# A channel shuffle on one core: tiles of 32 KB a partition, permuted in place through PSUM, from one pool of six buffers

## The chip, the cores and the metric

One core of a Trainium2 chip. The metric is device time in microseconds (us) of one execution. Each kernel was run several times; medians are quoted. All profiled runs are with granted clock 1.00. The kernel's tiles lie in two on-chip memories, SBUF and PSUM, over 128 partitions. "Row" below means one pixel of 256 channels, 1 KB in float32. A tile of q rows a partition holds 128 x q rows, so a tile of 24 rows is 3 MB and one of 8 rows is 1 MB.

## The reference

```python
batch, h, w, c = 16, 64, 64, 256
groups = 8
x = x.reshape(batch, h, w, groups, c // groups)
x = x.transpose(0, 1, 2, 4, 3)          # (group, channel) -> (channel, group)
return x.reshape(batch, h, w, c).astype(np.float32)
```

Inside every row of 256 values, an 8 x 32 matrix is transposed. 67.1 MB are read and 67.1 MB written. Rows are independent, so a kernel may place them on partitions as it likes.

## The kernel before

SyncE issues the loads. VectorE permutes the first half of the rows of a tile, and ScalarE the second half, from an input tile to an output tile in SBUF. ScalarE's queue issues the stores. There are four input and four output buffers of 24 KB a partition.

```python
_SIZES = [24] * 21 + [8]
_IN_BUFS = 4
_OUT_BUFS = 4
_SHARES = (("vector", 1), ("scalar", 1))
# ... cut: set-up, rows(), permute() ...
    for q in _SIZES:
        in_tile = in_pool.tile([P, biggest * c], F32, name="in_tile")
        nc.sync.dma_start(out=in_tile[:, : q * c], in_=rows(x_flat, first, q))
        out_tile = out_pool.tile([P, biggest * c], F32, name="out_tile")
        # ... cut: VectorE permutes the first half, ScalarE the second ...
        nc.scalar.dma_start(out=rows(out_flat, first, q), in_=out_tile[:, : q * c])
        first += P * q
```

`rows()` gives each partition q consecutive rows. So for each partition a DMA moves one contiguous run of q KB, and the trace records each run as one packet: in each of the two queues 2,688 packets of 24,576 B and 128 of 8,192 B, for 21 tiles of 24 rows and one of 8. The counts of the queues further below also hold 352 records of 4 B, of 9 ns each.

## Time and profile before

| | before |
|---|---|
| time, median of 3 | 317.53 us |
| span of the profiled run | 316.0 us |
| packets of loads and stores, share of 16 engines' time | 49.8% + 49.3% |
| VectorE, ScalarE busy | 65.3, 118.9 us |
| last load landed, last store issued | 302.4, 304.3 us |

From the page: busy time of the engines; the DMA row, which has the busy tenths of the DMA engines in 40 slices of the span (9 is 90% or more); and the queues (packets, MB, share). Queue q1 carries the loads and q10 the stores.

```profile
DVE 65.3 (21%) x22; ACT 118.9 (38%) x23; POOL 0.2 (0%) x4
...
DMA  8999999999999999999999999999999999999996
...
q1 hardware_dynamic: 3168, 67.11, 49.8%
q10 hardware_dynamic: 3168, 67.11, 49.3%
```

DMA is full from the second slice to the last but one. No compute engine is near that. From the view of waits (us in total, times, longest):

```profile
DVE out_tile L51 <- DMA in_tile<-in_x_dram: 238.3, 22, 11.6
ACT out_tile L49 <- DMA in_tile<-in_x_dram: 184.6, 22, 9.2
```

Both compute engines wait for loads only. From the groups by shape (count, then busy us, mean ns of one; then idle us before them and its releaser):

```profile
L49 ACT COPY out_tile<-in_tile 128x3072 f32<-128x3072 f32 x21 | 115.7, 5510 | 180.3 <-DMA in_tile<-in_x_dram 180.3
L51 DVE COPY out_tile<-in_tile 128x3072 f32<-128x3072 f32 x21 | 64.2, 3058 | 231.6 <-DMA in_tile<-in_x_dram 231.6
L49 ACT COPY out_tile<-in_tile 128x1024 f32<-128x1024 f32 x1 | 1.9, 1937 | 4.3 <-DMA in_tile<-in_x_dram 4.3
...
L51 DVE COPY out_tile<-in_tile 128x1024 f32<-128x1024 f32 x1 | 1.1, 1095 | 6.7 <-DMA in_tile<-in_x_dram 6.7
```

From the difference of the two shapes, a strided copy costs VectorE (3,058 - 1,095) / 2,048 = 0.96 ns an element and ScalarE (5,510 - 1,937) / 2,048 = 1.74 ns. By windows (start:end and length in us, busy us of each engine and instructions in brackets, clock, DMA share, GB/s):

```profile
core 0: us, DVE busy (x) ACT busy (x) POOL busy (x), PEclk, DMA share, GB/s
60.00:280.00 220.00, 47.01 (x16) 83.46 (x16) 0.00 (x0) 1.00 1.00 432
...
302.00:308.00 6.00, 1.09 (x1) 1.94 (x1) 0.00 (x0) 1.00 1.04 446
308.00:310.00 2.00, 0.00 (x0) 0.00 (x0) 0.00 (x0) 1.00 0.97 418
310.00:312.00 2.00, 0.00 (x0) 0.00 (x0) 0.00 (x0) 1.00 0.85 360
312.00:314.00 2.00, 0.00 (x0) 0.00 (x0) 0.00 (x0) 1.00 0.87 369
314.00:316.00 2.00, 0.00 (x0) 0.00 (x0) 0.00 (x0) 1.00 0.01 4
```

The middle moves 432 GB/s with DMA at 1.00.

### The profile page before, as it was taken

How to read it: one execution, taken by the hardware profiler on the slowest of the kernel's cores; microseconds unless marked ns; L12 is line 12 of the kernel's file. 1: busy time of each engine (PE TensorE's matmuls, PEld its weight loads, DVE VectorE, ACT ScalarE, POOL GpSimd, SP SyncE). 2: the span in 40 equal slices, each digit the busy share in tenths (PEclk: the TensorE clock that was granted, in tenths of full speed). 3: DMA queues.
4: the chain of work that ended last, by engine and by line, in shares of the span. 5: the costliest groups of instructions: out<-in, count | busy, mean ns of one | idle time of the engine just before them, and what ended most of it. 6: DMA issues, size and time to landing. Idle time of an engine off the chain costs nothing.

```text
span 316.0 us, 236 instructions
## 1 busy us (share of the span) xinstructions
DVE 65.3 (21%) x22; ACT 118.9 (38%) x23; POOL 0.2 (0%) x4
## 2 busy tenths in 40 slices
DVE  0440321303030303113030303031220303030310
ACT  1681624425160606243351606061533426060620
POOL 0000000000000000000000000000000000000000
DMA  8999999999999999999999999999999999999996
GB/s 302 439 395 426 426 445 432 420 442 439 417 439 445 417 436 442 426 426 445 426 423 445 439 414 442 442 417 439 442 421 432 442 420 432 442 429 429 421 446 291
DMA packets 6337, 134.23 MB, mean 425 GB/s; under 512 B 704, under 2 KB 704, under 8 KB 704
## 3 DMA queue, kind: packets, MB, share of 16 engines
q1 hardware_dynamic: 3168, 67.11, 49.8%
q10 hardware_dynamic: 3168, 67.11, 49.3%
q14 instruction: 1, 0.01, 0.0%
HBM read 67.11 MB, written 67.11 MB: 425 GB/s over the span
## 4 chain that ended last, share of the span: by engine, by line
another core or an unknown queue 43%; DMA 32%; ACT 20%; ACTq 1%; issue 0%
DMA in_tile<-in_x_dram 32%; ACT out_tile L49 20%; ACTq L66 1%; ACTq L49 0%
## 5 line engine op out<-in xcount | busy, mean ns | idle before, releaser
L49 ACT COPY out_tile<-in_tile 128x3072 f32<-128x3072 f32 (+1 forms) x22 | 117.7, 5348 | 184.6 <-DMA in_tile<-in_x_dram 184.6
L51 DVE COPY out_tile<-in_tile 128x3072 f32<-128x3072 f32 (+1 forms) x22 | 65.3, 2968 | 238.3 <-DMA in_tile<-in_x_dram 238.3
L49 ACT ACT_TABLE_LOAD x1 | 1.3, 1283 | 0.7 <-PEq L84 0.7
L84 POOL MEMSET const-bfloat16-1.0<- 128x1 bf16 x1 | 0.1, 102 | 0.0
L84 POOL MEMSET const-uint8-127<- 128x1 uint8 x1 | 0.1, 102 | 0.0
L84 POOL MEMSET const-float32-1.0<- 128x1 f32 x1 | 0.1, 99 | 0.0
L84 POOL MEMSET const-float32-0.0<- 128x1 f32 x1 | 0.1, 98 | 0.2 <-issue 0.2
## 6 DMA issues: line engine op xcount, KB each, us to landing
in_tile<-in_x_dram SPq DMA_DIRECT2D x21, 3072.0 KB, 52.6
out_dram<-out_tile ACTq DMA_DIRECT2D x21, 3072.0 KB, 20.2
in_tile<-in_x_dram SPq DMA_DIRECT2D x1, 1024.0 KB, 47.9
out_dram<-out_tile ACTq DMA_DIRECT2D x1, 1024.0 KB, 10.4
```

Of the source, the lines that this page charges most:

```text
L49: nc.scalar.copy(out=dst, in_=src)
L51: getattr(nc, engine).tensor_copy(out=dst, in_=src)
L66: nc.scalar.dma_start(out=rows(out_flat, first, q), in_=out_tile[:, : q * c])
L84: nc = _bacc.Bacc("TRN2", target_bir_lowering=False, num_devices=1)
```

## The change

The intent: larger tiles, hence fewer and larger DMAs, in the same 192 KB of SBUF a partition (8 x 24 and 6 x 32). For that each tile is permuted in place: VectorE permutes eight rows at a time into PSUM, and ScalarE copies them back over the input. An 8-row tile at the start and small ones at the end are to shorten head and tail.

```diff
-_SIZES = [24] * 21 + [8]
-_IN_BUFS = 4
-_OUT_BUFS = 4
+_SIZES = [8] + [32] * 14 + [24, 8, 8, 8, 8]
+_BUFS = 6
-_SHARES = (("vector", 1), ("scalar", 1))
+_PIECE = 8
 # ... cut: pools; permute() removed; the order of instructions is now that of the program ...
     for q in _SIZES:
-        in_tile = in_pool.tile([P, biggest * c], F32, name="in_tile")
-        nc.sync.dma_start(out=in_tile[:, : q * c], in_=rows(x_flat, first, q))
-        out_tile = out_pool.tile([P, biggest * c], F32, name="out_tile")
-        # ... cut ...
-        nc.scalar.dma_start(out=rows(out_flat, first, q), in_=out_tile[:, : q * c])
+        buf = pool.tile([P, biggest * c], F32, name="buf")
+        nc.sync.dma_start(out=buf[:, : q * c], in_=rows(x_flat, first, q))
+        for k in range(0, q, _PIECE):
+            piece = buf[:, k * c : (k + _PIECE) * c]
+            bounce = psum.tile([P, _PIECE * c], F32, name="bounce")
+            nc.vector.tensor_copy(
+                out=bounce.rearrange("p (i j g) -> p i j g", j=CPG, g=G),
+                in_=piece.rearrange("p (i g j) -> p i j g", g=G, j=CPG),
+            )
+            nc.scalar.copy(out=piece, in_=bounce)
+        nc.scalar.dma_start(out=rows(out_flat, first, q), in_=buf[:, : q * c])
```

Tiles are numbered from 0: tile 0 has 8 rows, tiles 1 to 14 have 32, tile 15 has 24, and tiles 16 to 19 have 8.

More of the change, by code (lines that the diff above doesn't have):

```diff
@@ L36 @@
     out_flat = out.rearrange("b h w c -> (b h w c)")
-    in_pool = ctx.enter_context(tc.tile_pool(name="in_pool", bufs=_IN_BUFS))
-    out_pool = ctx.enter_context(tc.tile_pool(name="out_pool", bufs=_OUT_BUFS))
+    pool = ctx.enter_context(tc.tile_pool(name="pool", bufs=_BUFS))
+    psum = ctx.enter_context(
+        tc.tile_pool(name="psum", bufs=2, space=bass.MemoryType.PSUM)
+    )
     def rows(flat, first, q):
         return flat[first * c : (first + P * q) * c].rearrange("(p f) -> p f", p=P)
-    def permute(engine, dst, src):
-        src = src.rearrange("p (i g j) -> p i j g", g=G, j=CPG)
-        dst = dst.rearrange("p (i j g) -> p i j g", j=CPG, g=G)
-        if engine == "scalar":
-            nc.scalar.copy(out=dst, in_=src)
-        else:
-            getattr(nc, engine).tensor_copy(out=dst, in_=src)
+    ctx.enter_context(tc.manual_schedule(engines=None))
     first = 0
     for q in _SIZES:
-        in_tile = in_pool.tile([P, biggest * c], F32, name="in_tile")
-        nc.sync.dma_start(out=in_tile[:, : q * c], in_=rows(x_flat, first, q))
-        out_tile = out_pool.tile([P, biggest * c], F32, name="out_tile")
-        at, total = 0, sum(n for _, n in _SHARES)
-        for k, (engine, n) in enumerate(_SHARES):
-            last = k == len(_SHARES) - 1
-            upto = q if last else min(q, at + -(-q * n // total))
-            if upto > at:
-                cols = slice(at * c, upto * c)
-                permute(engine, out_tile[:, cols], in_tile[:, cols])
-            at = upto
-        nc.scalar.dma_start(out=rows(out_flat, first, q), in_=out_tile[:, : q * c])
+        buf = pool.tile([P, biggest * c], F32, name="buf")
[6 more added lines that the diff above has]
+                in_=piece.rearrange("p (i g j) -> p i j g", g=G, j=CPG),
+            )
+            nc.scalar.copy(out=piece, in_=bounce)
+        nc.scalar.dma_start(out=rows(out_flat, first, q), in_=buf[:, : q * c])
         first += P * q
```

## The prediction

> **What bounds the kernel now.** The 16 DMA engines do, from end to end. The page's DMA row reads 9 in all slices but the first and last; the two queues' packets fill 49.8% + 49.3% = 99.1% of the 316.0 us span (queue table). By windows, 60 to 280 us moves 432 GB/s at DMA share 1.00, while VectorE is busy 47 and ScalarE 83 of those 220 us. Both idle only for loads (238 and 185 us, view of waits). [...]
>
> The packet records show the rest: a 24,576 B packet takes 912 ns, an 8,192 B one 309 ns. Hence 36.8 ns per KB (435 GB/s over 16 engines) plus about 7.5 ns a packet. The traffic, 67.1 MB in and 67.1 MB out, needs 308.7 us at that slope. Per engine: 352 packets x 7.5 ns = 2.6 us and 44 completion packets x 9 ns = 0.4 us. About 1.7 us is lost in slow packets at the start and where the first stores join. [...]
>
> **What the change does.** The bytes stay.
> - DMA: 20 loads and 20 stores instead of 22 and 22; 320 packets an engine instead of 352. Saves 32 x 7.5 + 4 x 9 = about 0.3 us, all on the path.
> - VectorE permutes everything: 64 pieces of 2,048 elements. Today (groups by form) 3,072 take 3,058 ns and 1,024 take 1,095: 0.96 ns an element. [...] I expect up to twice today's slope: 2.2 to 4.1 us a piece, best guess 4.0, in all about 255 us. Off the path: a 32-row tile costs DMA 2 x 8 x 1.21 = 19.4 us, VectorE 16 us.
> - ScalarE: strided copy (1.75 ns an element) becomes a contiguous one from PSUM, about 1.9 us a piece, 120 us in all; today 119. Off the path.
> - The latency from landing to store rises from 5.5 to about 18 us a full tile. It holds one of six buffers; the other five keep a load or a store queued, so DMA should not starve.
> - Head: the 8-row first tile lets stores begin near 10 us instead of 17, but loads already fill DMA then.
> - Tail: 24, 8, 8, 8, 8 keeps the last permutations (about 4 + 2 us each) under stores still queued; worth a few tenths at most.
>
> **Sum.** 317.5 - 0.3 (packets) - 0.1 (tail) = **317.1 us**, range 315.7 to 319.3. Chances: faster by over 2% 0.01, within 2% 0.95, slower 0.04.
>
> **What would show each step.** DMA share 1.00 and 432 to 434 GB/s in the middle; 32 KB packets near 1,214 ns; VectorE busy 140 to 260 us; ScalarE 115 to 130 us; the DMA row 9 throughout.
>
> **What would make it wrong.** A VectorE piece above about 4.8 us: VectorE would then need over 308 us and bound the kernel. Load and store queues both empty at times (DMA digit under 9 mid-run), because six shared buffers and the long landing-to-store latency starve them: slower. Faster would need a packet cost or a start loss that I have misread.

The range for a piece on VectorE (one to two times today's 0.96 ns an element, best guess 4.0 us), and with it 140 to 260 us, was the author's guess, and so was the 1.9 us of ScalarE: no run had shown a copy into or out of PSUM yet. The loss in slow packets comes to 1.6 us an engine by the packet records (their time beyond 912 and 309 ns each).

## More of the kernel before

The end is the part to remember: DMA stays near full until about 314 us. The timeline shows why (start, length, engine and line, operation; in brackets the idle time before it and its releaser; ACTq is ScalarE's queue issuing a DMA):

```profile
302.35 1.94 ACT L49 COPY out_tile<-in_tile 128x1024 f32<-128x1024 f32 x1 [4.29 <-DMA in_tile<-in_x_dram]
302.41 2.25 ACTq L66 DMA_DIRECT2D out_dram<-out_tile  x2
302.52 1.09 DVE L51 COPY out_tile<-in_tile 128x1024 f32<-128x1024 f32 x1 [6.70 <-DMA in_tile<-in_x_dram]
```

The last load lands at 302.35 us. After 1.94 us of ScalarE its store can be issued (the two issues in the line of 302.41 are those of the last two tiles, the later one at 304.3 us). By the packet records some 5 MB of stores are still to be moved when the load lands and some 4 MB when that store is issued, so the wait for the last tile's permutation is hidden.

## The result, and the profile after

| | before | after |
|---|---|---|
| time, median of 6 | 317.56 us | 319.85 us (319.63 to 320.71) |
| ratio of fast runs, 95% interval | | 1.0074 (1.0061 to 1.0087) |
| span of the profiled run | 316.0 us | 317.8 us |
| packets' share | 49.8% + 49.3% | 49.4% + 49.0% |
| VectorE, ScalarE busy | 65.3, 118.9 us | 228.2, 120.7 us |
| last load landed, last store issued | 302.4, 304.3 us | 307.6, 313.2 us |

A ratio here is the mean time of one kernel's fast runs over that of the other's in the same rounds, so it is not quite the ratio of the medians.

The change is 0.7% slower: inside "the same within 2%", but above the top of the predicted range, 319.3 us. The same lines of the page:

```profile
DVE 228.2 (72%) x64; ACT 120.7 (38%) x65; POOL 0.2 (0%) x4
...
DMA  8999999999999999999999999999999999999995
...
q1 hardware_dynamic: 2880, 67.11, 49.4%
q10 hardware_dynamic: 2880, 67.11, 49.0%
```

The packets took less time than before: 98.4% of 317.8 is 312.7 us an engine, against 99.1% of 316.0, or 313.2 us. So DMA did its work about 0.5 us faster (0.3 us was forecast), and the span is still 1.8 us longer. DMA stood still for about 2.3 us more than before. The groups and the waits:

```profile
L54 DVE COPY bounce<-buf 128x2048 f32<-128x2048 f32 x64 | 228.2, 3633 | 83.0 <-DMA buf<-in_x_dram 83.0
L58 ACT COPY buf<-bounce 128x2048 f32<-128x2048 f32 x64 | 119.4, 1865 | 186.9 <-DVE bounce L54 186.9
```

```profile
ACT buf L58 <- DVE bounce L54: 186.9, 64, 9.7
DVE bounce L54 <- DMA buf<-in_x_dram: 83.0, 18, 7.9
```

A piece takes VectorE 3,633 ns and ScalarE 1,865 ns. VectorE still waits for loads for 83 us in all, so it does not bound the kernel. The windows show where DMA stood still:

```profile
60.00:280.00 220.00, 166.27 (x47) 86.55 (x47) 0.00 (x0) 1.00 1.00 434
...
302.00:308.00 6.00, 3.96 (x2) 1.62 (x1) 0.00 (x0) 1.00 1.00 423
308.00:310.00 2.00, 2.00 (x1) 0.24 (x1) 0.00 (x0) 1.00 0.75 315
310.00:312.00 2.00, 1.26 (x1) 0.71 (x1) 0.00 (x0) 1.00 0.80 328
312.00:314.00 2.00, 0.00 (x0) 1.16 (x1) 0.00 (x0) 1.00 0.00 0
314.00:316.00 2.00, 0.00 (x0) 0.00 (x0) 0.00 (x0) 1.00 1.05 434
316.00:318.00 2.00, 0.00 (x0) 0.00 (x0) 0.00 (x0) 1.00 0.22 90
```

In the middle DMA moves 434 GB/s, a little more than before. From 308 us on its share is 0.75, 0.80 and then 0.00: from 312 to 314 us nothing is moved at all. Adding 1 - share times the length over all windows from 290 us to the end gives 4.6 us of standing still, against 2.5 us before (the last window counted to the end of the span; the window from 290 to 302 us, with shares 0.96 and 0.99, is counted in this and not shown). The timeline of the end:

```profile
294.22 3.60 DVE L54 COPY bounce<-buf 128x2048 f32<-128x2048 f32 x1 [7.92 <-DMA buf<-in_x_dram]
...
302.75 3.60 DVE L54 COPY bounce<-buf 128x2048 f32<-128x2048 f32 x1 [4.93 <-DMA buf<-in_x_dram]
...
307.64 3.62 DVE L54 COPY bounce<-buf 128x2048 f32<-128x2048 f32 x1 [1.29 <-DMA buf<-in_x_dram]
308.27 0.34 ACTq L59 DMA_DIRECT2D out_dram<-buf  x1
311.29 1.86 ACT L58 COPY buf<-bounce 128x2048 f32<-128x2048 f32 x1 [3.05 <-DVE bounce L54]
313.19 0.34 ACTq L59 DMA_DIRECT2D out_dram<-buf  x1
```

The last load lands at 307.6 us, 5.3 us later than before. Then come VectorE (3.62 us), ScalarE (1.86 us) and the store's issue at 313.19 us. The store of the tile before was issued at 308.27 us and has only 1 MB, so the stores run dry while the last tile is permuted.

Why does the last load land so late? The packet records of the trace are of each packet its start, length, queue and size. Packets of 8, 24 and 32 KB take 309, 912 and 1,213 ns (medians) in both directions. From first packet to last, the loads of tiles 16 to 19 (1 MB each) take 11.6, 11.3, 8.9 and 5.2 us, one right behind the other. Estimated from these times, a 1 MB load of 8 packets an engine would need 8 x 0.309 = 2.5 us with the engines to itself, and 4.9 us with half of their time. (The last 1 MB store, with no other transfer beside it, took 2.7 us.) Between 270 and 290 us after the first load packet, loads started 224 packets and stores 208, but these were 1.8 MB of loads and 6.7 MB of stores: in this stretch the two queues got nearly equal numbers of packets, not equal bytes. One 8 KB packet for each 32 KB packet would give 8 x (0.309 + 1.213) = 12.2 us for a 1 MB load, again an estimate from the packet times. That is near the 11.6 us seen.

### The profile page after: what moved, and what is told of

Its sections match the earlier page's. It is cut to its first block, busy times and chain, and to the rows that moved or that the text cites. A ratio compares the mean times of both kernels' runs of the same rounds, so it can differ in the third digit from the quotient of the medians.

```text
span 317.8 us, 277 instructions
## 1 busy us (share of the span) xinstructions
DVE 228.2 (72%) x64; ACT 120.7 (38%) x65; POOL 0.2 (0%) x4
## 3 DMA queue, kind: packets, MB, share of 16 engines
q1 hardware_dynamic: 2880, 67.11, 49.4%
q10 hardware_dynamic: 2880, 67.11, 49.0%
## 4 chain that ended last, share of the span: by engine, by line
DVE 59%; DMA 23%; another core or an unknown queue 15%; issue 1%; ACT 1%; SPq 0%; DVEq 0%
DVE bounce L54 59%; DMA buf<-in_x_dram 13%; DMA out_dram<-buf 9%; ACT buf L58 1%; SPq L50 0%; DVEq L54 0%
## 5 line engine op out<-in xcount | busy, mean ns | idle before, releaser
L54 DVE COPY bounce<-buf 128x2048 f32<-128x2048 f32 x64 | 228.2, 3633 | 83.0 <-DMA buf<-in_x_dram 83.0
L58 ACT COPY buf<-bounce 128x2048 f32<-128x2048 f32 x64 | 119.4, 1865 | 186.9 <-DVE bounce L54 186.9
```

Of the source, the lines that this page charges most:

```text
L54: nc.vector.tensor_copy(out=bounce.rearrange("p (i j g) -> p i j g", j=CPG, g=G), in_=piece.rearrange("p (i g j) -> p i j g", g=G, j=CPG),)
L58: nc.scalar.copy(out=piece, in_=bounce)
```

## The experiments

Three theories were set against each other.

- Theory A: loads and stores take turns packet by packet. The small tiles at the end are loaded in 8 KB packets against 32 KB store packets, so they come in slowly while the stores are used up quickly. The last load lands late, the stores run dry, and the permutation of the last tile (3.6 + 1.9 us) stands bare.
- Theory B: the long way from landing to store (about 16 us for a full tile), with six shared buffers, starves DMA in the middle, or the longer serial permutation alone is the cause.
- Theory C: the last load is late because its buffer comes free late. Its load is issued only at 280.2 us, when the store of tile 13 has landed.

Each kernel is the changed one with the edit shown, unless said otherwise. Times are medians, and the ratio in brackets is to the kernel before in the same rounds.

### Stores of tiles 13 to 15 cut into DMAs of 8 rows

```diff
-        nc.scalar.dma_start(out=rows(out_flat, first, q), in_=buf[:, : q * c])
+        dst = rows(out_flat, first, q)
+        step = _PIECE if t >= 13 else q
+        for k in range(0, q, step):
+            cut = slice(k * c, (k + step) * c)
+            nc.scalar.dma_start(out=dst[:, cut], in_=buf[:, cut])
```

> The change as it is, but the stores of tiles 13, 14 and 15 are issued as DMAs of 8 rows, so their packets are 8 KB like those of the last four loads. Theory A (packet-fair sharing delays the last small loads behind 32 KB store packets, so the last load lands at 307.6 us, the stores run dry and DMA idles about 2.2 us before the last store): loads of tiles 16 to 19 take about 5 us of traffic each instead of 9 to 11.5, the last load lands before 297 us, no DMA gap near 312 us, time 319.85 - 2.7 + 0.6 (64 more packets an engine at 7.5 ns, and more completions) = about 317.8. Theory B (only the length of the serial permutation at the end, or starvation in the middle by the long landing-to-store latency): the gap stays, time 320 to 320.5.

Measured 317.93 us (1.0012). By the packet records the last four loads took 4.7, 5.1, 5.8 and 5.3 us instead of 11.6 to 5.2, and DMA has share 1.02 from 312 to 314 us where the changed kernel has 0.00. The loss is gone, as theory A has it. One thing had not been foreseen: ScalarE was held up once for 24.5 us. The view of waits puts this to the landing of a load; the reading is that a store had to wait until a load on the same completion counter had landed (see the run with a buffer of its own for the last tile). So the experiment was repeated in a cleaner form at the end of this section.

### The last tile permuted by one VectorE copy in SBUF

```diff
+        if t == len(_SIZES) - 1:
+            last = last_pool.tile([P, q * c], F32, name="last")
+            nc.vector.tensor_copy(out=<last, permuted>, in_=<buf, strided>)
+            nc.scalar.dma_start(out=rows(out_flat, first, q), in_=last)
+            break
```

> The change as it is, but the last 8-row tile is permuted by one VectorE copy into an 8 KB SBUF buffer of its own and stored from there. Chain from the last landing to the store shortens from 5.5 us (3.63 + 1.86) to about 2.1 us. Theory A and the serial-chain rival alike: the 2.2 us DMA gap before the last store closes, time about 317.6; the last load still lands near 307.5. If the loss sits in the middle or the start (starvation by six shared buffers), nothing changes: 319.8.

Measured 317.57 us (1.0005). The last load still lands at 307.8 us, but its store is issued at 309.91 us instead of 313.19, and DMA is at share 0.96 from 312 to 314 us. So all of the loss sits between the last landing and the last store. Starvation in the middle is excluded. The groups of this run also show what the way through PSUM costs, with the same shape and the same pattern:

```profile
L63 DVE COPY bounce<-buf 128x2048 f32<-128x2048 f32 x63 | 224.6, 3633 | 82.0 <-DMA buf<-in_x_dram 82.0
...
L54 DVE COPY last<-buf 128x2048 f32<-128x2048 f32 x1 | 2.1, 2069 | 1.2 <-DMA buf<-in_x_dram 1.2
```

2,069 ns from SBUF to SBUF, 3,633 ns from SBUF to PSUM.

### Old flow, new sizes

The kernel before, with `_SIZES = [8] + [32] * 14 + [24, 8, 8, 8, 8]` and 3 + 3 buffers of 32 KB.

> The old flow (separate input and output pools, permutation split between VectorE and ScalarE) with the new tile sizes, 3 + 3 buffers of 32 KB. Theory A: loads are released by permutation, not by stores, so the small last loads are queued early and the last one lands with more than 10 us of stores still to do; no gap; about 317.3 (fewer packets). If the new sizes are by themselves the cause (small loads against large store packets, whatever the flow): a gap at the end and 319 to 320.

> The same kernel as the old flow with the new sizes, which gave 317.5, 317.6, 319.5, 319.6, 320.8 and 322.8 us. If the small loads at the end leave the order of the last transfers to chance, the spread comes again: some runs at 317.5, some 2 to 5 us above, and a profile of a long run shows the last load or the last store starting late. If it was one chip's or one hour's: all within 0.3 us of 317.5.

Theory A's forecast in the first expectation (about 317.3 us, no gap) was a miss. The six runs took 317.55 to 322.78 us, median 319.55 (1.0054, interval 1.0027 to 1.0081). Run again on another occasion, they spread again, as the second expectation allowed: 317.41 to 323.41 us, median 318.22 (1.0016, interval 0.9997 to 1.0035). The longest run of each six is classed as slow, being over 1.5% above the fastest, although its granted clock is 1.00. It counts in the median and not in the ratio, and without it the second median is 317.67 us. In the first profile, of a run of 317.63 us, the last load lands as late as in the changed kernel, at 308.4 us, but only 1.94 us of ScalarE follow; DMA has share 0.69 from 308 to 310 us and 1.02 right after. In the second, of a run of 318.76 us, it lands at 309.4 us, and the share from 308 to 310 us is 0.52. That is 0.3 us more of standing still there, out of 1.1 us between these two runs; the rest is not explained. The kernel before spread over only 0.7 us in the rounds of both occasions. So the new sizes put the old flow on the edge too: the last load is late in both flows. That it depends on the run whether the stores last until it is permuted is likely, but not shown: no profile caught a run above 319 us, so what the longest runs lost is open.

### New flow, old sizes

`_SIZES = [24] * 21 + [8]`, eight buffers of 24 KB.

> The new flow (permutation through PSUM in place, one pool) with the old sizes, 21 tiles of 24 rows and one of 8, eight buffers of 24 KB. Theory A: the last load waits for a store to land and for the tile before it on VectorE (10.9 us), only one small load meets large packets; gap at the end of 0 to 2 us, 317.5 to 319.5. If the flow's long latency starves DMA in the middle: DMA share under 1.00 between 60 and 280 us and over 320.

Measured 317.60 us (0.9998), at the lower end of the forecast. Share 1.00 and 432 GB/s from 60 to 280 us. Its last store is issued at 302.0 us. ScalarE also waited for the landing of loads here, four times and 55.3 us in all (by the author's reading stores held up by completion counters, as told further below), and even that cost nothing. So the slow permutation through PSUM costs nothing by itself with eight buffers of 24 KB. Six buffers of 32 KB, the other half of theory B, are in the next run.

### No small tiles at the end

`_SIZES = [8] + [32] * 15 + [24]`.

> The new flow with sizes 8, 15 x 32, 24: no small loads at the end, so no 8 KB load packets against 32 KB store packets. Theory A: last load (24 rows) lands near 286 us, its three pieces and its store issue are done near 303 us, while stores still fill DMA; no gap; 272 packets an engine instead of 320 save another 0.4 us: 317.0. If what costs is the long serial permutation after the last landing (now 10.7 + 1.9 us instead of 5.5), the loss grows: 321 or more.

Measured 317.07 us (0.9980, interval 0.9968 to 0.9993). The last load lands at 289.9 us. Its tile needs 10.7 us of VectorE and 1.9 of ScalarE, more than twice the chain of the changed kernel, and its store is issued at 302.55 us under stores that last until the end. From its timeline:

```profile
289.92 10.70 DVE L54 COPY bounce<-buf 128x2048 f32<-128x2048 f32 x3 [2.76 <-DMA buf<-in_x_dram]
...
302.55 0.34 ACTq L59 DMA_DIRECT2D out_dram<-buf  x1
```

The longer chain does no harm, because the load comes early. With six buffers of 32 KB DMA has share 1.00 and 434 GB/s from 60 to 280 us, so theory B falls. This kernel has the lowest median, though the intervals of the two other kernels without small tiles overlap with its own. It beats the kernel before by 0.5 us and the changed one by 2.8, and it differs from the latter in the size list only.

### The last VectorE copy done twice

```diff
-            nc.vector.tensor_copy(...)
+            for _ in range(2 if t == len(_SIZES) - 1 else 1):
+                nc.vector.tensor_copy(...)
```

> The change as it is, with the last tile's VectorE copy done twice (same result). If the chain after the last landing is exposed, all of the added 3.6 us shows: 319.85 + 3.6 = 323.4, and the DMA gap before the last store grows from 2 to 5.6 us. If something else sets the end, under 1 us shows.

Measured 323.55 us (1.0192). The added 3.6 us appear as 3.7, and the gap is where it should be:

```profile
312.00:314.00 2.00, 1.97 (x2) 0.00 (x0) 0.00 (x0) 1.00 0.48 197
314.00:316.00 2.00, 2.00 (x1) 0.00 (x0) 0.00 (x0) 1.00 0.00 0
316.00:318.00 2.00, 0.24 (x1) 1.73 (x1) 0.00 (x0) 1.00 0.00 0
318.00:320.00 2.00, 0.00 (x0) 0.14 (x1) 0.00 (x0) 1.00 0.54 225
```

DMA does nothing from 314 to 318 us (the profile is of the longest run, 324.61 us). The chain after the last landing is exposed one to one, as the second experiment had it from the other side. It is exposed only because the load is late, as the run without small tiles shows.

### A buffer of its own for the last tile, and for the last four

```diff
-        buf = pool.tile([P, biggest * c], F32, name="buf")
+        if t < len(_SIZES) - 1:            # second kernel: - 4, and _BUFS = 5
+            buf = pool.tile([P, biggest * c], F32, name="buf")
+        else:
+            buf = last_pool.tile([P, q * c], F32, name="last")   # second kernel: bufs=4
```

> The change as it is, but the last 8-row tile has an SBUF buffer of its own, so its load need not wait for the store of tile 13 (to 280.2 us) and is issued with the one before it, near 268 us. Theory A says the load queue was never empty and its small packets are what is slow: the last load still lands near 307 us, time 319.8 as the change. Rival C (the load is late because its buffer comes free late): it lands some 10 us earlier, no gap, 317.5.

Measured 317.31 us (0.9991): by its number a win for theory C and a miss for A. The trace shows that something else moved as well. In the trace of the changed kernel the landings of its 40 loads and stores are counted on eight semaphores, five transfers on each, and none of the 32 later transfers was issued before the one before it on its semaphore had landed. Tile 9's store was held up by that: its last piece was copied back by 172.94 us, but it was issued at 176.13, just after tile 10's load, on the same semaphore, had landed at 176.06. In the run here something like it befell the store of tile 13. Its last piece was copied back by 251.7 us, but it was issued at 269.10 us, and the view of waits puts a wait of ScalarE of 17.9 us before its next copy to the landing of a load. The author's reading, not shown by itself, is that moving the last load forward shifted the turns by one, so that this store fell on the counter of tile 15's load. Meanwhile, by the packet records, the loads had DMA to themselves, and two of the small ones passed in 3.4 and 2.8 us. The two that again met 32 KB store packets took 12.4 and 15.8 us, although both had been issued by 268.51 us. So the run does not test theory C cleanly, and in the part that does it speaks for A. Its sister was meant to avoid this:

> The change's sizes with five buffers of 32 KB and four of 8 KB for the last four tiles: the last four loads are free to be issued together, near 230 us, right behind tile 15's load. No store waits for another transfer's counter for long here, as it did by accident in the run with one buffer for the last tile. Theory A: the loads still run one after another against 32 KB store packets, 9 to 12 us each from about 270 us; the last lands at 303 to 308 us; 319.3 to 319.9. Rival C: the last load lands before 297 us, 317.5.

Measured 318.20 us (1.0020), between the two forecasts. All of the last four loads were issued by 234.5 us. By the packet records they still took 12.0, 12.0, 11.1 and 8.0 us, and the last landed at 306.15 us, against 307.64: issuing them 46 us earlier gained 1.5 us. But here too a store went out late, contrary to the expectation: that of tile 12, issued at 251.5 us instead of about 231 (231.06 in the changed kernel). The author puts this to a counter as well. So the 1.5 us cannot be given to the early issue with certainty.

### Rows of 40

`_SIZES = [8] + [40] * 12 + [24]`, five buffers of 40 KB.

> The new flow with sizes 8, 12 x 40, 24 and five buffers of 40 KB: 224 packets an engine. Theory A with the packet cost of 7.5 ns: 96 x 7.5 = 0.7 us less than the change from packets and no gap of 2.2 us: 316.7 to 317.0. If fewer, larger buffers starve DMA: share under 1.00 in the middle, 319 or more.

Measured 317.23 us (0.9986), 0.2 us above the forecast. Share 1.00 and 433 GB/s in the middle. Going from 32 to 40 rows gains nothing that these runs can tell from the kernel without small tiles.

### Stores of tiles 13 to 15 in 8 KB packets, all else equal

The result is wrong on purpose. The three stores write their 8-row blocks in another order, so each is still one DMA, and only its packets are smaller (the page counts 3,904 packets in the store queue, against 2,880 in the changed kernel).

```diff
+        if 13 <= t <= 15:
+            n = q // _PIECE
+            nc.scalar.dma_start(
+                out=out_flat[first * c : (first + P * q) * c].rearrange("(a p f) -> p a f", p=P, a=n),
+                in_=buf[:, : q * c].rearrange("p (a f) -> p a f", a=n),
+            )
```

> Wrong result on purpose: the stores of tiles 13, 14 and 15 write their 8-row blocks in another order, so that each store is still one DMA but in packets of 8 KB. All instructions, waits and completion counters stay as in the change (in the first try of this the three stores were 11 DMAs, and a store had to wait for another transfer's counter). Theory A (packets take turns, so an 8 KB load packet waits out a 32 KB store packet): loads 16 to 19 land about 5 us apart instead of 9 to 12, the last before 297 us instead of 307.6; no gap; 319.85 - 2.7 + 0.5 (64 more packets an engine) = 317.7. Rival C (the late release of the last buffer, at 280 us): nothing moves earlier, 320.3.

Measured 317.41 us (0.9993), 0.3 us better than forecast. By the packet records the last four loads took 5.5, 5.5, 5.6 and 5.3 us. The timeline of the last tile, and the windows that were nearly empty in the changed kernel:

```profile
295.08 3.60 DVE L54 COPY bounce<-buf 128x2048 f32<-128x2048 f32 x1 [4.79 <-DMA buf<-in_x_dram]
...
300.61 0.34 ACTq L66 DMA_DIRECT2D out_dram<-buf  x1
```

```profile
308.00:310.00 2.00, 0.00 (x0) 0.00 (x0) 0.00 (x0) 1.00 1.03 434
310.00:312.00 2.00, 0.00 (x0) 0.00 (x0) 0.00 (x0) 1.00 0.99 418
312.00:314.00 2.00, 0.00 (x0) 0.00 (x0) 0.00 (x0) 1.00 0.88 373
```

The last load lands at 295.08 us, 12.6 us earlier, its store is issued at 300.61 us, and DMA stays full. The buffer of the last tile came free later than in the changed kernel (its load was issued at 285.69 us, not 280.20), and yet the loss is gone. So the late release, theory C, does not make the loss by itself; the size of the packets on the other queue does. Whether the late release adds to the loss while the packets differ in size stays open: the run with four small buffers, in which a store also went out late, was 1.65 us faster than the changed kernel.

### Old flow, no small tiles

The kernel before with `_SIZES = [8] + [32] * 15 + [24]`, 3 + 3 buffers.

> The old flow (two pools, 3 + 3 buffers of 32 KB) with sizes 8, 15 x 32, 24. If the sizes at the end are what costs and the flow itself gives nothing: as the new flow with these sizes, 317.0 to 317.2. If the new flow has a gain of its own hidden under the tail's loss: 317.5 or more.

Measured 317.17 us (0.9985), with a spread of 0.4 us. This is the same as the new flow with these sizes. The gain of 0.4 to 0.5 us belongs to the sizes. With these sizes the way through PSUM and the single pool neither give nor take anything that these runs can tell.

## Why the prediction was right or wrong

- Right: DMA bounds the kernel, at 432 to 434 GB/s with share 1.00 in the middle, before and after.
- Right: the gain from fewer packets. A 32 KB packet was forecast at 1,214 ns and measured 1,213. The forecast saving was 0.3 us, and the time of the packets, by their rounded shares, fell by 0.5 us.
- Right: VectorE and ScalarE stay off the path in the middle. VectorE was busy for 228 us (forecast 140 to 260, best guess 255), ScalarE for 121 (115 to 130). A piece took 3.6 us where 4.0 was guessed. ScalarE took 1.74 ns an element for its strided copy before, and 1,865 / 2,048 = 0.91 ns (the whole copy, fixed part included) for the contiguous one from PSUM; that the stride makes the difference was not tested by itself.
- Right: six shared buffers do not starve DMA. That the 8-row first tile gives nothing (its store was issued at 11.1 us) was not tested by itself.
- Wrong, and nearly all of the error of 2.75 us: the step "Tail: 24, 8, 8, 8, 8 keeps the last permutations (about 4 + 2 us each) under stores still queued; worth a few tenths at most". In the sum it was -0.1 us. Measured, the end of the changed kernel has about 2.1 us more of standing still than before, and the runs that remove it (a shorter last chain, store packets of 8 KB, no small tiles) are 1.9 to 2.8 us faster. The length of the permutation was sized well (forecast 4 + 2 us, measured 3.6 + 1.9). What failed is "under stores still queued". The prediction takes this for granted and never says how loads and stores share DMA. With equal shares it would have held: where the store packets were of 8 KB too, a 1 MB load took 5.5 us and the last permutation was hidden. But the two queues moved nearly the same number of packets (224 and 208 in 20 us), so loads in 8 KB packets against stores in 32 KB packets got a fifth of the bytes (1.8 of 8.5 MB). The last load landed at 307.6 us, the stores before it had run out by 311.8 us (packet records), and the last one was issued at 313.2 us.
- A hint of this was in the trace of before: its last load, in 8 KB packets against 24 KB stores, took 9.4 us for 1 MB, where turns packet by packet would give 8 x (0.309 + 0.912) = 9.8 us (an estimate from the packet times).
- Of the signs that were named as making the prediction wrong, none occurred. The tail was not among them in this form.

## What to carry to other kernels

When loads and stores share DMA engines, compare the sizes of the runs a partition moves, not only the bytes: in 20 us here the queue with 8 KB runs moved 1.8 MB while the one with mostly 32 KB runs moved 6.7 MB. Small tiles at the end of a stream, meant to shorten the tail, can therefore arrive too late if large stores are still running: here the last load landed at 307.6 us, 5.3 us later than before. Two cures worked here: no small tiles at the end (317.07 us), or those stores cut into runs of the same size (317.93 us). In a kernel bound by DMA, check at the end that the last landing plus its chain of work is over before the queued stores are; the windows of the last 10 us show it at once.
